# Setup work moved between the projections of a hybrid attention layer

## The chip, the cores and the metric

The kernel runs on one core of a Trainium2 chip. The metric is the time of one launch on the device in microseconds (us), as the median of several runs. A profile of one execution stands beside it.

Of the core's engines, TensorE (PE in the profile; PEld is its weight load) multiplies matrices and writes to PSUM, VectorE (DVE) and ScalarE (ACT) read PSUM and do the arithmetic between, GpSimd (POOL) takes part of the subtractions, and SyncE (SP) issues all transfers, in order, on one queue.

## The reference, cut to what matters

One layer of a streaming encoder on 2048 prompt tokens and 32 sample tokens of width 1024, in float32:

```python
z = rmsnorm(x, g_attn) @ w_in            # qa, ka, va (group A), qb, kb, vb (group B): 512 columns each
# A: differential attention, 4 heads, two maps of 64; bias from a T5 table, chunk-causal mask
lam = exp(sum(q1 * k1)) - exp(sum(q2 * k2)) + lam_init
oa = (softmax(s1 + bias) - lam * softmax(s2 + bias)) @ va
# B: band attention, 8 heads of 64; own chunk and 8 before; bias from a clipped table
ob = softmax(sb + band_bias) @ vb
h = x + concat(subnorm(oa), rmsnorm(ob)) @ w_out
h = h + square(relu(rmsnorm(h) @ w_up)) @ w_down
h = h + sigmoid(h @ w_ple_gate) * (p @ w_ple_proj)   # p: per-layer input, 256 wide
y = rmsnorm(h, g_final)
```

The keys and values are outputs too.

## The kernel before

Every float32 matmul is made of three with operands split in a high and a low part (`mm3`, lines 190 to 192): high by high, low by high and high by low. ScalarE or VectorE casts the high part, VectorE or GpSimd subtracts for the low one (`split`, L169, L171, L154, L164).

The tokens are cut into four blocks of 512 (the last has the 32 sample tokens too), in two halves. The normalised, transposed tokens of a block lie in two tiles, `aH` and `aL`. `prep` makes them, one token tile of 128 at a time: a load, a sum of squares, transposes (`rp`, `xp`), eight scalings (L345), a split.

`proj(half, grp, ..., vs, gs)` is a generator. It first makes the value columns in two pieces (`vs`: tiles `vps`, `vraw`, `vhl`), then for each of the four column groups (`gs`) the queries and the keys (`qps`, `qh`, `ql`, `kr`), and stores all of it to scratch in HBM (`vSa`, `vSb`, `qS`, `kS`). The key rows of the output are transposed back (`ktp`). The `qh` and `ql` tiles have two buffers each; the PSUM tiles of the projections, two as well.

The setup consists of three functions. `lam` works out lambda. `biases` multiplies one-hot tables (`oa`, `ob`) with the bias tables (`ta`, `tb`) into two rows (`pa`, `pb`), stores them (`ra`, `rb`) and spreads each row over 128 partitions by twelve copies from HBM to HBM (`dba`, `dbb`); attention loads its bias tiles from there. `prep_p` loads the per-layer input of each block (`pn`), transposes it on TensorE (`ppt`), splits it (`pph`, `ppl`, in the same buffers as `qh` and `ql`) and stores it to `pS`.

Then comes the first attention part: `attn_a` on the pairs of query tiles (0, 1), for each of the four heads, and again on (2, 3): two passes. Each step has score matmuls (`s`), a softmax on VectorE and ScalarE (`e`), transposes of the weights (`tpp`) and output matmuls (`o`). After it in the text come the group B projections of block 0, of block 1 with `prep` of block 2 woven in, the band attention `attn_b` (`sb`, `eb`, `tpb`, `ob`) on the first half, the projections of block 2 with `prep` of block 3, and so on; last the output projection, the MLP and the gate, which reads `pS`.

The order in which the engines meet all this isn't the order of the text. A scheduler with a timeline of its own sorts the instructions when the program is built: what stands earlier in the text has priority, and what stands later fills in where the earlier work waits by that timeline. So projections from further down run between the steps of attention. The order is fixed when the program runs; each engine takes its instructions strictly in that order. Pools with a fixed number of buffers set when a tile can be written again.

Of the kernel before, what the change touches and what calls it, by code (L numbers as in the profile page):

```python
# [41 lines left out]
HALVES = [(0, 1), (2, 3)]  # L42
# [40 lines left out]
def drain(gen):  # L83
    for _ in gen:
        pass
# [13 lines left out]
def weave(main, side, step, i=0, n=1):  # L99
    for _ in main:  # L100
        if i % step == 0:
            for _ in range(n):
                next(side, None)
        i += 1
    drain(side)
# [28 lines left out]
class Kern:  # L134
# [640 lines left out]
    def prep_p(self, sg, wk, ps):  # L775
        nc, a = self.nc, self.a
        for b in range(4):
            t0 = 512 * b
            n = BN[b]
            pn = wk.tile([P, 5, DPLE], F32, tag="pn", bufs=2, name="pn")  # L780
            self.dma(pn[:, :4], a["p_prompt"][0, 0, t0 : t0 + 512].rearrange("(i p) c -> p i c", p=P))
            if b == 3:
                self.dma(pn[:SS, 4], a["p_sample"][0, 0])
            for k in range(2):
                hi = sg.tile([P, BLK], F32R, tag="qh", bufs=2, name="pph")
                lo = sg.tile([P, BLK], F32R, tag="ql", bufs=2, name="ppl")
                pieces = [(0, 512)] + ([(512, SS)] if b == 3 else [])
                for c0, w in pieces:
                    tp = ps.tile([P, 512], F32, tag="tp", name="ppt")
                    for i in range(max(w // P, 1)):  # L790
                        m = min(w, P)
                        nc.tensor.transpose(
                            tp[:, P * i : P * i + m], pn[:m, c0 // P + i, P * k : P * k + P], self.ident[:m, :m]
                        )
                    nc.scalar.activation(hi[:, c0 : c0 + w], tp[:, :w], AF.Copy)
                    nc.vector.tensor_tensor(
                        lo[:, c0 : c0 + w], tp[:, :w], hi[:, c0 : c0 + w].bitcast(F32), op=ALU.subtract
                    )
                self.dma(self.pS[:, 0, k, t0 : t0 + n], hi[:, :n])
                self.dma(self.pS[:, 1, k, t0 : t0 + n], lo[:, :n])  # L800

    def raw_o(self, wk, k, t0, n):
        t = wk.tile([P, BLK], F32, tag="tmp", bufs=4, name="oraw")[:, :n]
        self.dma(t, self.oT[:, k, t0 : t0 + n])
        return t
# [290 lines left out]
    def run(self):  # L1096
        tc, nc, a = self.tc, self.nc, self.a
        with ExitStack() as top:

            def opened(stack, name, bufs, space=None, side="left"):  # L1100
                kw = {} if space is None else {"space": space}
                return stack.enter_context(
                    tc.tile_pool(name=name, bufs=bufs, side=side, reuse_waits="tile", **kw)
                )
# [5 lines left out]
            mm = opened(top, "mm", MM, PSUM)  # L1110
            tp = mm
            psx = ExitStack()
            ps_s = opened(psx, "pss", 5 - MM, PSUM, "right")
            ps_t = opened(psx, "pst", 2, PSUM, "right")
# [4 lines left out]
            sg = opened(s12, "sg", 2)  # L1119
            self.consts(cp)  # L1120
            with ExitStack() as x:
                pp = opened(x, "pp0", 3, side="right")
                acts = {b: self.actpair() for b in HALVES[0]}
# [1 line left out]
                    drain(self.prep(b, acts, pp, ps_s, "s"))  # L1125
            ppx = ExitStack()
            pp = opened(ppx, "pp", 1)
            drain(self.proj(HALVES[0], 0, acts, sg, mm, Rings((ps_t, "tp"))))
            with ExitStack() as x:
                wk = opened(x, "setup", 1, side="right")  # L1130
                self.lam(cp, wk)
                self.biases(wk, ps_t)
                self.prep_p(sg, wk, ps_t)
            self.small = True
            mark = tc.tile_snap_priority()
            with ExitStack() as x:
# [47 lines left out]
            wk = opened(sq_, "wk", 1)  # L1184
# [41 lines left out]
            wk = opened(top, "wk4", 1)  # L1226
# [79 lines left out]
```

## Time and profile before

| | us |
|---|---|
| median of three runs | 3257.93 |
| lowest, highest | 3256.70, 3264.15 |
| profiled execution | 3256.49 |
| its span | 3254.6 |

The profiled execution has its own time, 1.9 us above the span that the engines' rows cover. Times of rows are us from the span's start. A row of a window gives each engine's busy time and number of instructions, then TensorE's granted clock (1.00 is full speed), the mean busy share of the 16 DMA engines and GB/s. A row of a timeline gives start, duration, engine, line and operation; in brackets stands the idle time ahead of it and what ended it. `out<-in` are the program's tile names. Matmuls are pipelined: the distance between the starts of two neighbours is what one costs, and the duration is longer.

### The profile page before, as it was taken

Reading aid. Unit: us, or ns where it says so; the run is one execution under the profiler, and the core shown is the slowest. Engines: PE = TensorE matmul, PEld = TensorE weight load, DVE = VectorE, ACT = ScalarE, POOL = GpSimd, SP = SyncE. Lnnn points to the kernel's source line nnn. Section 1 sums busy time; section 2 is a strip of 40 time slices with the busy share of each in tenths; the row PEclk is TensorE's granted clock in tenths of the full one; section 3 lists DMA queues with packets and bytes.
Section 4 is the critical chain, followed back from the end, with each engine's and each line's share of the span. In section 5 each row is a group of like instructions: output and inputs, shape, how many; then the busy total and the mean of one; then the engine's idle time right before and its main releaser. Section 6 shows DMA issues by size and latency. Waiting matters only on the chain. (4 is left out here: it accounts for less than half of the span.)

```text
span 3254.6 us, 51557 instructions
## 1 busy us (share of the span) xinstructions
PE 3076.7 (95%) x17881; PEld 2692.7 (83%) x17881; DVE 1557.3 (48%) x3952; ACT 1693.7 (52%) x3717; POOL 1706.8 (52%) x2515
## 2 busy tenths in 40 slices
PE   6998999899999999999999999989899999999998
PEld 6877789789987887878788788868789999999988
DVE  5116786544465554676664565625442232223235
ACT  4226666776666765676665566544443222322245
POOL 5446766233245544565655455676854333433387
PEclk9999999999999999999999999999999999999999
DMA  7488786786788654554644544347531111111133
GB/s 232 165 259 246 226 244 206 213 259 202 215 239 229 187 146 118 152 156 138 199 122 135 137 123 136 121 143 233 150 113 46 46 46 46 46 46 46 47 94 103
DMA packets 519085, 489.02 MB, mean 150 GB/s; under 512 B 37885, under 2 KB 414017, under 8 KB 518825
## 3 DMA queue, kind: packets, MB, share of 16 engines
q1 hardware_dynamic: 518824, 485.73, 50.9%
q8 instruction: 142, 2.33, 0.3%
q14 instruction: 119, 0.97, 0.1%
HBM read 379.06 MB, written 110.49 MB: 150 GB/s over the span
## 5 line engine op out<-in xcount | busy, mean ns | idle before, releaser
L164 POOL TENSOR_TENSOR wl<-wr,wh 128x256 fp32r<-128x256 f32 x936 | 695.2, 774 | 489.4 <-ACT wh L169 453.1
L169 ACT ACTIVATE wh<-wr 128x1024 fp32r<-128x1024 f32 x338 | 357.2, 1057 | 598.5 <-PE dps L191 298.9
L971 DVE TENSOR_TENSOR h<-h,dps 128x512 f32<-128x512 f32 (+1 forms) x640 | 373.0, 585 | 575.0 <-PE dps L192 562.7
L154 POOL TENSOR_TENSOR wl<-wr,wh 128x256 fp32r<-128x256 f32 x416 | 301.8, 757 | 401.2 <-ACT wh L169 386.9
L190 PE MATMUL dps<-uh,wh 128*128 128x512 f32 (+1 forms) x1280 | 458.2, 358 | 7.1 <-DVE h L971 5.8
L190 PE MATMUL ups<-cH,wh 128*128 128x512 f32 (+1 forms) x1280 | 452.7, 354 | 5.7 <-ACT relu L936 4.5
L191 PE MATMUL ups<-cL,wh 128*128 128x512 f32 (+1 forms) x1280 | 451.5, 353 | 1.5 <-POOL cL L154 1.2
L192 PE MATMUL ups<-cH,wl 128*128 128x512 f32 (+1 forms) x1280 | 450.8, 352 | 0.0
L192 PE MATMUL dps<-uh,wl 128*128 128x512 f32 (+1 forms) x1280 | 450.1, 352 | 0.0
L191 PE MATMUL dps<-ul,wh 128*128 128x512 f32 (+1 forms) x1280 | 449.3, 351 | 0.0
L154 POOL TENSOR_TENSOR ul<-relu,uh 128x136 fp32r<-128x136 f32 (+1 forms) x320 | 198.9, 643 | 171.0 <-ACT uh L169 166.7
L190 PEld LDWEIGHTS dps<-uh,wh 128*128 128x128 f32 x1280 | 241.6, 189 | 39.7 <-DVE h L971 10.2
L190 PEld LDWEIGHTS ups<-cH,wh 128*128 128x128 f32 x1280 | 241.1, 188 | 38.6 <-ACT relu L936 4.7
L191 PEld LDWEIGHTS ups<-cL,wh 128*128 128x128 f32 x1280 | 241.6, 189 | 33.0 <-POOL cL L154 2.0
L192 PEld LDWEIGHTS dps<-uh,wl 128*128 128x128 f32 x1280 | 240.9, 188 | 33.6
L192 PEld LDWEIGHTS ups<-cH,wl 128*128 128x128 f32 x1280 | 241.3, 189 | 30.0
L191 PEld LDWEIGHTS dps<-ul,wh 128*128 128x128 f32 x1280 | 241.9, 189 | 26.5
L190 PE MATMUL qps<-aH,wh 128*128 128x512 f32 (+1 forms) x640 | 229.7, 359 | 11.0 <-ACT kr L432 3.4
L192 PE MATMUL qps<-aH,wl 128*128 128x512 f32 (+1 forms) x640 | 228.0, 356 | 0.0
L191 PE MATMUL qps<-aL,wh 128*128 128x512 f32 (+1 forms) x640 | 227.9, 356 | 0.0
L567 PE MATMUL s<-ka,q 128*128 128x256 f32 (+4 forms) x784 | 191.7, 346 | 30.8 <-DMA ka<-kS 10.1
L581 ACT ACTIVATE e<-s,nm 128x512 f32<-128x512 f32 (+3 forms) x256 | 154.9, 611 | 80.3 <-DVE nm L573 69.4
(218 smaller groups left out, 7075.0 us busy)
## 6 DMA issues: line engine op xcount, KB each, us to landing
wr<-w_up SPq DMA_DIRECT2D x96, 512.0 KB, 4.2
wr<-w_down SPq DMA_DIRECT2D x96, 512.0 KB, 3.8
wr<-w_in SPq DMA_DIRECT2D x74, 512.0 KB, 5.1
q<-qS SPq DMA_DIRECT2D x256, 128.0 KB, 4.3
v<-vSa SPq DMA_DIRECT2D x64, 512.0 KB, 3.9
ka<-kS SPq DMA_DIRECT2D x32, 512.0 KB, 7.7
wr<-w_out SPq DMA_DIRECT2D x32, 512.0 KB, 4.7
wr<-w_ple_gate SPq DMA_DIRECT2D x32, 512.0 KB, 4.4
```

The lines of the kernel that those rows point to most:

```text
L154: nc.gpsimd.tensor_tensor(out[:, sl], a[:, sl], b[:, sl], op=op)
L164: nc.gpsimd.tensor_tensor(out[:, sl], a[:, sl], b[:, sl], op=op)
L169: nc.scalar.activation(hi, raw, AF.Copy)
L190: nc.tensor.matmul(ps, lh, rh, start=start and i == 0, stop=False)
L191: nc.tensor.matmul(ps, lh, rl, start=False, stop=False)
L192: nc.tensor.matmul(ps, ll, rh, start=False, stop=stop and i == n - 1)
L567: nc.tensor.matmul(s, q[:, m, hl, P * qi : P * qi + nr], kt[:, m, k0 : k0 + n], start=hl == 0, stop=hl == 1)
L581: nc.scalar.activation(dst, src, AF.Exp, bias=nmx, accum_out=z[:nr, m, bi : bi + 1])
L971: nc.vector.tensor_tensor(hv, hv, ps, op=ALU.add)
```

## The change

`proj` of group A on the first half is cut in two: the value columns first, then `lam` and `biases`, then the query and key columns with `prep_p` woven in. For that `prep_p` becomes a generator that yields after each of its eight pieces, and `weave` advances it once for every second step of `proj`. Both calls of `proj` share one ring of PSUM tiles, and the pool `setup` is opened ahead of them.

```diff
                 self.dma(self.pS[:, 0, k, t0 : t0 + n], hi[:, :n])
                 self.dma(self.pS[:, 1, k, t0 : t0 + n], lo[:, :n])
+                yield
...
             pp = opened(ppx, "pp", 1)
-            drain(self.proj(HALVES[0], 0, acts, sg, mm, Rings((ps_t, "tp"))))
             with ExitStack() as x:
                 wk = opened(x, "setup", 1, side="right")
+                ring = Rings((ps_t, "tp"))
+                drain(self.proj(HALVES[0], 0, acts, sg, mm, ring, gs=()))
                 self.lam(cp, wk)
                 self.biases(wk, ps_t)
-                self.prep_p(sg, wk, ps_t)
+                weave(self.proj(HALVES[0], 0, acts, sg, mm, ring, vs=()), self.prep_p(sg, wk, ps_t), 2)
```

Nothing is added to or taken from the arithmetic or the transfers.

## The prediction

> **What bounds the kernel now.** I read the page first, then the table of windows of four microseconds around the place that is changed, then TensorE's and SyncE's rows in order of time there, and last the windows of the stages that follow.
>
> ```profile
> span 3254.6 us, 51557 instructions
> PE 3076.7 (95%) x17881; PEld 2692.7 (83%) x17881; DVE 1557.3 (48%) x3952; ACT 1693.7 (52%) x3717; POOL 1706.8 (52%) x2515
> ```
>
> TensorE is busy 95% of the span, and the change neither adds nor removes an instruction: on every engine the changed program holds the same instructions in another order. So time can only come from TensorE's idle stretches, from its clock, and from how well other work covers them. Around 208 us both are bad:
>
> ```profile
> core 0: us, PE busy (x) PEld busy (x) DVE busy (x) ACT busy (x) POOL busy (x), PEclk, DMA share, GB/s
> 192.00:200.00 8.00, 8.00 (x71) 8.00 (x70) 2.06 (x4) 3.86 (x6) 4.03 (x6) 1.00 0.63 213
> 208.00:212.00 4.00, 1.25 (x11) 1.05 (x9) 0.69 (x1) 1.19 (x2) 0.00 (x0) 1.00 1.06 392
> 212.00:216.00 4.00, 1.70 (x8) 1.32 (x8) 0.99 (x2) 0.00 (x0) 0.00 (x0) 0.73 1.09 362
> 216.00:220.00 4.00, 2.69 (x6) 2.15 (x7) 0.63 (x1) 2.04 (x4) 2.16 (x4) 0.50 1.11 344
> 220.00:224.00 4.00, 4.00 (x17) 3.25 (x16) 1.72 (x3) 1.81 (x3) 4.00 (x7) 0.92 0.98 361
> 248.00:252.00 4.00, 3.49 (x9) 2.80 (x10) 2.02 (x8) 3.26 (x8) 1.72 (x3) 0.58 1.07 249
> ```
>
> The transfers fill the DMA engines (share 1.06 to 1.11), TensorE starves, and then runs at half its clock. Its own rows show both:
>
> ```profile
> 208.85 0.28 PE L191 MATMUL vps<-wl,aH 128*128 128x256 f32 x1
> 208.97 0.27 PE L192 MATMUL vps<-wh,aL 128*128 128x256 f32 x1
> 213.58 1.70 PE L792 MATMUL ppt<-ident,pn 128*128 128x128 f32 x8 [4.33 <-DMA pn<-p_prompt]
> 217.31 0.80 PE L190 MATMUL qps<-aH,wh 128*128 128x512 f32 x1 [2.03 <-ACT vraw L383]
> 218.33 0.63 PE L192 MATMUL qps<-aH,wl 128*128 128x512 f32 x1
> 218.76 0.63 PE L190 MATMUL qps<-aH,wh 128*128 128x512 f32 x1
> 221.02 0.40 PE L190 MATMUL qps<-aH,wh 128*128 128x512 f32 x1
> 221.26 0.39 PE L191 MATMUL qps<-aL,wh 128*128 128x512 f32 x1
> ```
>
> Two waits, 4.33 us for the third load of the per-layer input and 2.03 us behind it; then two 512-wide matmuls stand 0.43 us apart, and from 221 us on 0.24 us. SyncE's rows say what filled the DMA engines:
>
> ```profile
> 58.66 0.45 SPq L145 DMA_DIRECT2D lv<-lambda_q  x1
> 65.19 0.35 SPq L145 DMA_DIRECT2D ob<-onehot_b  x1
> 68.97 0.56 SPq L145 DMA_DIRECT2D pn<-p_prompt  x1
> 195.36 5.41 SPq L145 DMA_DIRECT2D dbb<-rb  x8
> 205.97 1.75 SPq L145 DMA_DIRECT2D pn<-p_prompt  x2
> ```
>
> The loads of lambda, the one-hot tables and the first input tiles already go out at 58 to 71 us: the scheduler had hoisted them. What comes late is what hangs on matmuls of low priority: the eight copies that spread the band bias, and the input loads and stores behind them.
>
> **The change part by part.** In the program's order the first bias matmul moves from TensorE's position 902 to 361, inside the first value projections; the 34 transposes move from 945-1132 to 486-880, in bursts of four or five between query and key projections; and the first score matmul of the first attention part moves from position 1195 to 943, as nothing stands ahead of it any more. That last shift reaches on: the order differs up to position 11376 of 17878.
>
> *The stall at 209 us* goes: 4.33 + 2.03 = 6.4 us of waiting, and the lost clock, (1-0.73)·4 + (1-0.50)·4 + (1-0.92)·4 = 3.4 us. Together -9.8 us. Late next is the start of attention, which then meets lighter transfers.
>
> *The moved work itself* costs the same wherever it stands, as TensorE is the bound at both places:
>
> ```profile
> 183.97 0.80 PE L260 MATMUL pa<-oa,ta 32*4 32x384 f32 x2
> 186.91 1.88 PE L268 MATMUL pb<-ob,tb 128*8 128x512 f32 x4
> 192.48 0.60 PE L792 MATMUL ppt<-ident,pn 128*128 128x128 f32 x4
> 100.00:125.00 25.00, 25.00 (x114) 20.28 (x113) 3.09 (x5) 5.71 (x9) 10.40 (x15) 1.00 0.46 156
> ```
>
> At its new place TensorE is never idle, the DMA share is 0.46, and ScalarE and VectorE (5.71 and 3.09 of 25 us) have room for the evictions: 0.
>
> [...] The rows of 192 to 200 us hold 16 such transposes among dense matmuls, at a granted clock of 1.00. [...]
>
> *The new wait.* SyncE issues in order, and it waits for the bias rows and for the copies before it goes on (columns: total us, times, longest; for `pS`, KB and median us to landing):
>
> ```profile
> SPq L145 <- DMA dbb<-rb: 5.3, 8, 1.2
> SPq L145 <- DMA ra<-va_row: 2.4, 1, 2.4
> pS<-pph SPq DMA_DIRECT2D x6, 256.0 KB, 7.2
> 246.89 0.60 ACT L426 ACTIVATE qh<-qps 128x512 fp32r<-128x512 f32 x1 [2.30 <-DMA qS<-qh]
> 248.51 0.79 PE L190 MATMUL qps<-aH,wh 128*128 128x512 f32 x1 [2.57 <-ACT kr L432]
> ```
>
> In the changed order the first two query stores stand right behind the eight copies. The projections would begin near 89 us, the copies go out to about 100 us, and a store behind them landed after 7.2 us before: near 107 us. The third eviction needs that buffer (two of them, now shared with the input's halves) at 101 us, and TensorE, with two PSUM tiles, at 107 us. So it is borderline: from 0 up to what such a wait cost at 248 us, 2.57 us plus (1-0.58)·4 = 1.7 us of clock, 4.3 us. I take +1, near the lower end, by the 0.4 us that the working leaves it.
>
> *The stall at 248 us*, that same 4.3 us, arose with the DMA engines full. It may or may not come back where attention now starts: -4.3 to 0; half of it, -2.1. [...]
>
> *The first attention part* (score, transpose and output matmuls of `attn_a` on the first half, with projections between) runs in two passes over the heads. In the changed order the first pass has 655 positions instead of 600 and holds one token tile of `prep` instead of four; the second has 1145 instead of 1302 and eight instead of five.
>
> ```profile
> 241.50:358.00 116.50, 101.13 (x600) 88.72 (x599) 81.72 (x290) 75.38 (x230) 79.59 (x116) 0.93 0.85 244
> 358.00:577.00 219.00, 208.30 (x1352) 187.94 (x1351) 151.27 (x438) 147.44 (x402) 149.58 (x209) 0.98 0.77 222
> 300.00:325.00 25.00, 19.47 (x146) 17.94 (x145) 20.24 (x79) 17.91 (x62) 18.79 (x28) 0.96 0.77 230
> 425.00:450.00 25.00, 23.11 (x177) 21.92 (x176) 22.98 (x74) 19.37 (x60) 16.99 (x24) 1.00 0.82 234
> L345 DVE SCALAR_TENSOR_TENSOR a<-xp,g_attn_s,rb 128x128 f32<-128x128 f32 x32 | 8.9, 338 | 0.1
> ```
>
> Lost in the first pass: 15.4 us idle and 0.07·116.5 = 8.2 us of clock, 23.5 us on 93 us of work, a rate of 0.25. In the second: 10.7 + 4.4 = 15.1 us on 204 us, 0.074. The changed passes hold 93·655/600 = 102 and 204·1145/1302 = 179 us of work. With both at the low rate they lose 21 us instead of 38.6 (-18), with both at the high one 71 (+32). VectorE is why I stay between: eight scalings of 0.338 us make a token tile cost it about 3 us, so its share falls in the first pass (72 of some 118 us, 61%) and rises in the second (from 69% to about 161 of 200 us, 80%). The window at 425 us, in the second pass, has VectorE at 92% and loses only 1.9 of 25 us; that at 300 us, 81% and 5.5 us. I take rates of 0.16 and 0.12, 16 + 21.5 = 37.8 us: -1.
>
> *The band attention* comes after. Its first heads run with no projection between them for 222 TensorE instructions in the present order and for 334 in the changed one (position 2944 to 3278).
>
> ```profile
> 601.00:653.00 52.00, 38.71 (x229) 30.50 (x228) 37.83 (x163) 46.63 (x129) 2.33 (x16) 0.93 0.82 219
> 653.00:700.00 47.00, 42.11 (x325) 39.98 (x325) 23.95 (x87) 36.62 (x77) 23.23 (x40) 1.00 0.97 279
> ```
>
> The first row is that bare stretch: ScalarE is busy 46.63 of 52 us and sets the pace, TensorE idles 13.3 us and loses 3.6 us of clock, 16.9 us; counting each of its 229 instructions at the 0.12 us that stands between two 256-wide matmuls (208.85 to 208.97 us), 24.5 us. The second row, with projections between, loses 4.9 us on 325. So 112 more bare instructions cost 112/222 of 16.9 to 24.5 us, less 1.7 us that they lost anyway: 6.8 to 10.7 us. I take +9.
>
> **The sum:** -9.8 + 1 - 2.1 - 1 + 9 = -2.9 us. The profiled execution took 3256.5 us (its span 3254.6), the median of three runs is 1.4 us above it; so 3253.6 there, 3255 on the median. A difference under 0.3% (9.8 us) is what a measurement of this kernel cannot tell from no change. With no term at an extreme this case reaches from 3246 to 3266.
>
> **The rivals.**
>
> *The second pass chokes (slower).* Eight token tiles in 1145 positions push VectorE so far that the second pass loses at the first one's rate: 45.4 instead of 21.5 us, +23.9; with the band's bare stretch at its upper end (+1.7) the sum is +22.7: 3281 on the median. It turns the case to measurably slower from a loss of about 34 us in that pass. For it: the window at 300 us, where 81% of VectorE goes with 5.5 us of 25 lost. Against it: the one at 425 us.
>
> *Everything that starves is gone (faster).* Without the full DMA engines and with three tiles fewer in the first pass both passes lose at the low rate (-18), the stall at 248 us goes whole (-4.3), no new wait comes, the band costs +6.8: -9.8 - 18 - 4.3 + 6.8 = -25 us, 3233; with the first pass at 0.12 instead of 0.074, 3238. For it: the first pass lost most right behind the 209 us stall. Against it: its DMA share stays 0.77 at 300 us, where no setup is left.
>
> *Nothing moves that mattered.* The loads were hoisted already; if the copies only stall another stretch by as much, 3258. Against it: the share of 0.46 at the new place.
>
> [...]
>
> **How the numbers follow.** The forecast's own case 0.36, nothing moves 0.05, everything gone 0.28, the second pass chokes 0.29, the clock 0.02. The first two are within 0.3%: 0.41; faster 0.28; slower 0.31. Faster and slower cases hold more than half together, so the range takes in most of both, up to about the rivals' values: 3238 to 3279.
>
> **What would show it.** Right: no wait of TensorE for the input load after 200 us; the copies of the band bias issued before 102 us; clock 1.00 and TensorE full from 90 to 190 us; the first score matmul near 192 us; a bare band stretch of about 78 us with ScalarE near 90%. Wrong: a wait above 2 us at 100 to 110 us or a half-clock stretch before 190 us; a second pass that loses over 34 us or under 14; a bare stretch that loses no more than 17 us.

## The result, and the profile after

The changed kernel takes 3282.31 us (median of 6 runs, 3274.69 to 3289.89); the kernel before, measured beside it, 3259.45 us (6 runs, 3256.50 to 3264.15). The ratio is 1.0069, its 95% interval 1.0052 to 1.0086: slower by about 0.7%, or 23 us. The forecast was 3255 us with a range of 3238 to 3279, so it was wrong, in sign too. The profiled execution took 3278.81 us. Its page:

```profile
span 3276.7 us, 51585 instructions
PE 3093.2 (94%) x17881; PEld 2705.0 (83%) x17881; DVE 1547.0 (47%) x3952; ACT 1695.1 (52%) x3717; POOL 1703.6 (52%) x2515
```

TensorE is busy 16.5 us longer with the same 17881 instructions and idle 5.6 us longer: 22.1 us in all. So part of the loss is clock, part idle time, and neither total says where. I therefore give each kernel a loss by stage: for each pair of neighbouring matmuls the distance of their starts, less the usual distance for that shape and tile (the lower quartile in the kernel before), added up where positive. It holds idle time and lost clock together. Losses by stage, in us, read in the profiled execution of each kernel (the experiments' kernels are explained below):

| | to the first score matmul | first attention part | band attention | second attention part and what is left of the MLP to position 11380 | rest | sum | span |
|---|---|---|---|---|---|---|---|
| before | 39.0 | 58.0 | 88.1 | 74.0 | 75.8 | 334.9 | 3254.6 |
| before, again | 40.8 | 57.2 | 90.0 | 73.2 | 76.1 | 337.3 | 3256.8 |
| after | 33.5 | 51.4 | 110.7 | 88.3 | 72.9 | 356.8 | 3276.7 |
| after, again | 32.0 | 56.7 | 109.0 | 88.3 | 73.0 | 359.0 | 3278.9 |
| e1 own buffers | 26.0 | 64.0 | 97.6 | 92.9 | 71.7 | 352.2 | 3270.7 |
| e2 bias only | 32.0 | 67.5 | 94.2 | 84.3 | 71.2 | 349.2 | 3268.1 |
| e3 input only | 38.1 | 67.5 | 98.9 | 80.3 | 75.7 | 360.5 | 3280.0 |
| e4 hold | 31.2 | 66.6 | 98.1 | 75.4 | 75.9 | 347.2 | 3267.7 |
| e5 caches moved | 41.8 | 69.3 | 96.7 | 83.1 | 71.5 | 362.4 | 3281.3 |
| e12 cover, before | 40.7 | 55.8 | 86.1 | 75.6 | 72.9 | 331.1 | 3248.4 |
| e16 cover, change | 29.3 | 55.1 | 92.0 | 75.2 | 72.1 | 323.7 | 3241.8 |

The sums follow the spans: after against before +21.9 by stages, +22.1 by span. Two executions of one kernel differ by up to 7 us in a stage. By the table the change wins 5.5 us (8.8 in the second pair of executions) ahead of the first score matmul and 6.6 (0.5) in the first attention part, and loses 22.6 (19.0) in the band attention and 14.3 (15.1) behind it. The table ends the first attention part at its last transposes of the weights; the output matmuls behind them, which lose 5.3 us after (5.2 again) and 0.3 before, stand in the band's column. With them where they belong, the first attention part is -1.5 us (+4.5) and the band +17.3 (+14.1).

Now the places, in order of time. Some of SyncE's rows of the changed kernel:

```profile
93.56 0.29 SPq L145 DMA_DIRECT2D rb<-vb_row  x1
95.19 1.12 SPq L145 DMA_DIRECT2D dbb<-rb  x2
97.00 4.04 SPq L145 DMA_DIRECT2D dbb<-rb  x6
102.26 0.33 SPq L145 DMA_DIRECT2D qS<-qh  x1
111.03 0.73 SPq L145 DMA_DIRECT2D qS<-qh  x1
```

The band bias now goes out at 94 to 101 us, and the first query store stands behind it, at 102.26 us. What waits for that store, by the rows of ScalarE and VectorE, and then by TensorE's:

```profile
110.41 0.60 ACT L426 ACTIVATE qh<-qps 128x512 fp32r<-128x512 f32 x1 [13.43 <-DMA qS<-qh]
111.26 0.69 DVE L427 SCALAR_TENSOR_TENSOR ql<-qps,qh 128x512 fp32r<-128x512 f32 x1 [13.46 <-DMA qS<-ql]
```

```profile
107.26 0.60 PE L792 MATMUL ppt<-ident,pn 128*128 128x128 f32 x4
112.01 0.80 PE L190 MATMUL qps<-aH,wh 128*128 128x512 f32 x1 [4.15 <-DVE ql L427]
```

The eviction needs the `qh` buffer, which is free only when the store has landed, some 8 us after its issue; TensorE stands for 4.15 us, and the windows of the changed kernel show the clock behind it, then the two passes of the first attention part and the bare stretch of the band (same columns as in the prediction):

```profile
104.00:108.00 4.00, 3.86 (x19) 2.93 (x17) 0.00 (x0) 0.00 (x0) 0.00 (x0) 1.00 0.96 311
108.00:112.00 4.00, 0.00 (x0) 0.00 (x0) 0.74 (x2) 1.08 (x2) 0.00 (x0) 0.78 1.06 364
112.00:116.00 4.00, 3.99 (x9) 3.17 (x10) 0.29 (x1) 1.06 (x1) 2.73 (x4) 0.50 1.09 335
116.00:125.00 9.00, 9.00 (x40) 7.36 (x39) 1.22 (x2) 2.63 (x4) 5.36 (x9) 0.94 0.80 263
125.00:190.00 65.00, 65.00 (x303) 52.67 (x303) 10.93 (x19) 17.09 (x29) 22.24 (x32) 1.00 0.63 215
...
208.00:212.00 4.00, 4.00 (x36) 4.00 (x36) 1.79 (x9) 3.03 (x10) 3.50 (x5) 1.00 1.07 271
197.40:304.30 106.90, 102.42 (x657) 93.03 (x655) 70.81 (x255) 71.26 (x213) 75.47 (x111) 0.97 0.89 252
304.30:515.30 211.00, 189.34 (x1148) 166.03 (x1146) 158.34 (x465) 146.75 (x407) 145.81 (x202) 0.96 0.75 217
...
554.60:632.10 77.50, 58.18 (x336) 44.94 (x334) 51.01 (x220) 64.33 (x166) 2.63 (x18) 0.96 0.83 222
```

The stall at 208 us is gone. The first pass idles 4.5 us instead of some 15, the second 21.7 us instead of 10.7; by spacing the first loses 13.9 us (32.9 before), the second 42.7 (25.2 before). The same stretches of the kernel before, cut at its own first and last instructions:

```profile
242.60:359.20 116.60, 101.23 (x601) 88.81 (x600) 81.72 (x290) 75.77 (x231) 80.80 (x117) 0.93 0.85 245
359.20:570.40 211.20, 200.50 (x1293) 180.37 (x1292) 150.54 (x436) 145.10 (x397) 144.59 (x202) 0.98 0.77 223
603.40:655.90 52.50, 38.25 (x225) 30.01 (x223) 36.54 (x161) 44.69 (x125) 2.03 (x14) 0.93 0.83 225
```

The bare stretch holds 94 score matmuls instead of 64 and takes 77.5 us instead of 52.5: 0.82 us for each in both, with ScalarE busy 83% and 85%. Its loss grows from 26.4 to 38.9 us, 0.41 us for each score in both. Ahead of it, from the last weight transposes of the first attention part on, 12.5 us are lost, where it was 4.4. Of these, 5.3 us lie in the last output matmuls of the first attention part: TensorE waits for the low half of the weights, because VectorE, ahead of it, waits for GpSimd, and half-clock matmuls follow (0.21 us apart instead of 0.12):

```profile
511.49 0.93 DVE L667 SCALAR_TENSOR_TENSOR os<-os,g_sub_s,rsy 128x256 f32<-128x256 f32 x1 [3.10 <-POOL rsy L204]
```

```profile
513.07 0.58 PE L654 MATMUL o<-pL,v 128*128 128x256 f32 x1 [3.53 <-DVE pL L647]
```

The same wait is 3.5 us in the second execution; in the second pass of the kernel before the longest wait of this kind is 0.3 us.

Behind the band the second attention part (positions 6870 to 10839 after, 7226 to 11223 before) takes as long as before with 28 fewer instructions, and after it 541 instructions of the MLP are left to position 11380 where there were 157. The windows of the second part and of that rest in the changed kernel, and TensorE's waits in the rest (total us, times, longest):

```profile
1187.90:2010.40 822.50, 782.80 (x3970) 659.84 (x3969) 496.50 (x1116) 511.87 (x1186) 445.31 (x633) 0.98 0.51 141
2010.40:2140.40 130.00, 124.63 (x543) 100.28 (x542) 48.52 (x71) 50.85 (x75) 86.72 (x123) 0.99 0.41 130
```

```profile
PE dps L190 <- ACT relu L937: 2.9, 1, 2.9
PE dps L190 <- DVE h L972: 2.2, 3, 0.8
```

And the two windows in the kernel before:

```profile
1258.40:2081.80 823.40, 787.77 (x3998) 663.18 (x3997) 502.86 (x1120) 515.72 (x1191) 451.70 (x639) 0.99 0.51 142
2081.80:2115.40 33.60, 33.60 (x160) 27.54 (x159) 20.34 (x30) 17.44 (x31) 27.83 (x41) 1.00 0.52 161
```

The MLP that is left alone waits for its own evictions (5.4 us idle where there was none; a loss of 10.5 instead of 1.5 us), and the attention part loses 78.0 instead of 72.7 us.

### The profile page after: what moved, and what is told of

It reads as the page before. It is cut to its first block, busy times and chain, and to the rows that moved or that the text cites. A ratio compares the mean times of both kernels' runs of the same rounds, so it can differ in the third digit from the quotient of the medians.

```text
span 3276.7 us, 51585 instructions
## 1 busy us (share of the span) xinstructions
PE 3093.2 (94%) x17881; PEld 2705.0 (83%) x17881; DVE 1547.0 (47%) x3952; ACT 1695.1 (52%) x3717; POOL 1703.6 (52%) x2515
## 5 line engine op out<-in xcount | busy, mean ns | idle before, releaser
L191 PEld LDWEIGHTS ups<-cL,wh 128*128 128x128 f32 x1280 | 242.1, 189 | 32.4 <-POOL cL L154 1.3
L573 DVE TENSOR_REDUCE nm<-s 128x1 f32<-128x512 f32 (+3 forms) x256 | 147.3, 587 | 106.3 <-PE s L567 105.5
```

The costliest lines, as they stand in the source:

```text
L191: nc.tensor.matmul(ps, lh, rl, start=False, stop=False)
L573: nc.vector.tensor_reduce(nmx, s, axis=AX.X, op=ALU.max, negate=True)
```

## The experiments

Theory A: the change is slow because attention starts ahead of its work, so that projections have already run when the band's first heads and the end of the second attention part need something to stand between. (A' in two expectations is A, whatever set the order off.) Theory B: the setup at its new place does the harm, by the wait that it adds at 110 us. Theory C: any reshuffling of this tuned order costs about as much, whatever is moved. Differences are against the kernel before, measured beside each run.

**e1, own buffers.** The changed kernel with the halves of the per-layer input out of the shared buffers:

```diff
-                hi = sg.tile([P, BLK], F32R, tag="qh", bufs=2, name="pph")
-                lo = sg.tile([P, BLK], F32R, tag="ql", bufs=2, name="ppl")
+                hi = wk.tile([P, BLK], F32R, tag="pph", bufs=2, name="pph")
+                lo = wk.tile([P, BLK], F32R, tag="ppl", bufs=2, name="ppl")
```

> The changed kernel, but the halves of the per-layer input get tiles of their own instead of sharing the two buffers of the query and key halves. Theory A (most of the added time comes from the order of the work after the setup: second pass of the first attention part, bare band stretch, second attention part): only the wait at 107 us and its half-clock stretch go, 4.15 + 3.4 = 7.5 us; about 3275 us, still slower than before by 15 us. Theory B (the setup at its new place does the harm, by its copies and shared buffers, and the later differences follow from it): about 3260 us.

3272.19 us (3269.16 to 3279.94), ratio 1.0051 [1.0033, 1.0069]. Its windows at the place of the wait:

```profile
104.00:108.00 4.00, 4.00 (x21) 3.28 (x20) 0.00 (x0) 1.09 (x2) 0.00 (x0) 1.00 1.03 330
108.00:112.00 4.00, 4.00 (x19) 3.19 (x18) 1.03 (x2) 0.00 (x0) 1.24 (x2) 1.00 1.10 363
112.00:116.00 4.00, 4.00 (x21) 3.31 (x20) 0.00 (x0) 2.43 (x3) 2.20 (x4) 1.00 1.08 339
```

The wait and its half clock are gone, and the first stage loses 7.5 us less (6.0 less than in the changed kernel's second execution): that is the price of the new wait. But 14 us stay, near what was given for A, so theory B holds for 10 of the 23 us at most.

**e2 and e3, one part each.** e2 moves only lambda and the bias, e3 only the per-layer input:

```diff
 # e2
-                weave(self.proj(HALVES[0], 0, acts, sg, mm, ring, vs=()), self.prep_p(sg, wk, ps_t), 2)
+                drain(self.proj(HALVES[0], 0, acts, sg, mm, ring, vs=()))
+                drain(self.prep_p(sg, wk, ps_t))
 # e3
+                weave(self.proj(HALVES[0], 0, acts, sg, mm, ring, vs=()), self.prep_p(sg, wk, ps_t), 2)
                 self.lam(cp, wk)
                 self.biases(wk, ps_t)
-                weave(self.proj(HALVES[0], 0, acts, sg, mm, ring, vs=()), self.prep_p(sg, wk, ps_t), 2)
```

> Lambda and bias tables go behind the first value projections, the per-layer input stays behind all of the projections. Its program order has the first score matmul at position 1174 (before 1195, changed 943) and a bare band stretch of 253 instructions (222, 334). Theory A: it stays near before, 3255 to 3268 us, since attention starts as late. Theory B: the eight copies stand ahead of the first query stores as in the changed kernel, so 3270 us or more.

> The per-layer input is woven into the query and key projections, lambda and bias tables stay behind them. First score matmul at position 1104, bare band stretch 266. Theory A: between the two kernels, about 3262 to 3272 us. Theory B: without the copies ahead of the query stores no wait near 107 us, so no slower than before, 3250 to 3260 us.

e2: 3274.02 us, 1.0054 [1.0037, 1.0070]; e3: 3285.04 us, 1.0086 [1.0069, 1.0103]. Alone they cost some 16 and 27 us, where both together cost 23: the parts do not add up. e2's time is the one given for B, and e3's is above both that were given, so neither theory foresaw this pair. Both lose in the first attention part (67.5 us against 58.0) and in the band.

**e4 and e6, the later order held.** In the changed kernel the projections of group B on block 0 are put ahead of the first attention part, which gives the band its old length (bare stretch of 226 instructions, against 222) and the second part its old end (position 11223); e6 has e1's buffers too.

```diff
+            drain(self.proj((0,), 1, acts, sg, mm, tp, gs=range(4)))
             for js in JA0:
...
-            drain(self.proj((0,), 1, acts, sg, mm, tp))
+            drain(self.proj((0,), 1, acts, sg, mm, tp, vs=(), gs=()))
```

> The changed kernel, with all group B projections of block 0 written ahead of the first attention part in the text instead of behind it. The setup stands as in the changed kernel, but the order from the band attention on is nearly that of before: first band matmul at position 3251 in both, bare stretch 226 against 222, the end of the second attention part at 11223 in both, and the same instructions in the same order from position 7975 on. Theory A: the later terms go; the setup's own net of about -3 to -5 us is left, so 3250 to 3262 us. Theory B: the setup is unchanged, so 3275 us or more.

> The hold kernel with buffers of their own for the input's halves. Theory A': the wait near 107 us and its half clock go, as in the kernel with own buffers, 6 us off the hold kernel's 3270: about 3264 us. [...]

e4: 3270.30 us, 1.0050 [1.0032, 1.0068]; e6: 3275.76 us, 1.0043 [1.0028, 1.0058]. With the old end of the second part its loss is the old one: 75.4 us to position 11380, 1.5 of it in the MLP left over. That part of A holds. But the first attention part, now with other projections in it, loses 66.6 us, and the bare stretch 32.4, so e4 lies between the two times given. e6 missed its time (3264 us): the wait at 107 us went, and the first attention part lost 72.8 us instead.

**e5, another reshuffle.** In the kernel before, setup untouched, only `caches` (the stores of the key and value outputs) moves up in the text, ahead of the first band attention:

```diff
+            self.caches(sg, tp)
             acts[3] = self.actpair()
...
-            self.caches(sg, tp)
```

> The kernel before, setup untouched, with the small step that reads the caches written ahead of the first band attention in the text instead of behind it. The order is that of before up to about position 2050; then it reshuffles, with the first band matmul at 3137 (before 3251) and a bare stretch of 256 instructions (222). Theory A' (the order of the later stages carries the loss, whatever set it off): slower than before by 6 to 16 us, most of it in the second pass, the bare stretch and the second attention part. Theory B (the setup's place carries it): within 5 us of before.

3285.76 us, before 3262.20, 1.0074 [1.0057, 1.0090]: as much as the change under study, and more than the 6 to 16 us expected. TensorE's order is the same up to position 2050; the table has +11 us in the first attention part, +9 in the band, +9 behind it. Its last band instruction stands at position 7103 instead of 7226 and the second part ends at 11082 instead of 11223: it is shifted as the changed kernel is, only less.

**e7 and e8, the two kernels once more**, for the repeatability of the stages.

> The changed kernel once more, for a second trace. If its losses by stage belong to its order, the second pass (about 43 us lost), the bare stretch (39) and the second attention part (88) come out within 5 us each again; if they are a matter of where the half-clock windows fall, one of them moves by more than 8 us.

> The kernel before once more, for a second trace. If its losses belong to its order, first attention part 58, bare stretch 26 and second attention part 74 us come out within 5 us each again; otherwise as for the changed kernel.

3281.07 and 3258.55 us. Their stage rows stand in the table. In the changed kernel's second execution the second pass of the first attention part loses 48.3 us, a little more than 5 us off the first, and the bare stretch 35.2; in that of the kernel before they lose 24.4 and 27.8.

**e9, e10, e11, the stall taken away in the kernel before.** e9 gives the input loads four buffers, e10 gives the halves own buffers as well (e1's edit), e11 these alone.

```diff
-            pn = wk.tile([P, 5, DPLE], F32, tag="pn", bufs=2, name="pn")
+            pn = wk.tile([P, 5, DPLE], F32, tag="pn", bufs=4, name="pn")
```

> The kernel before, with four buffers instead of two for the loads of the per-layer input; nothing is moved in the text. All four loads then stand at 69 to 80 us in SyncE's order, and the later order stays close to that of before (first score matmul 1200 against 1195, first band matmul 3251, bare stretch 226 against 222, the same from position 7975 on). If the stall at 209 us is what there was to win, and the order what there was to lose: the 4.33 us wait and its half clock go, 6 to 10 us, less up to 3 us for two loads of 512 KB more in the full stretch at 70 to 80 us: about 3252 us against 3259. If any new order loses 10 to 20 us: 3262 us or more.

> The same with buffers of their own for the input's halves; the order is that of before from position 3814 on, and 0.986 of the positions between 3251 and 11376 hold the same instruction. The waits on the shared buffers at 215 and 248 us (2.03, 2.57 us) can go too: 3248 to 3254 us. If the first attention part's order alone decides, it may lose up to 10 us there instead: 3260 us.

> The kernel before with the input's halves in buffers of their own, two input loads at a time as before. Order as before from position 3814 on. The wait for the input load at 209 us stays; the waits on shared buffers go: 3255 to 3261 us. With the order of the first attention part against it, up to 3268 us.

3269.20 us (1.0034 [1.0021, 1.0047]), 3268.21 (1.0030 [1.0018, 1.0041]) and 3279.54 (1.0064 [1.0049, 1.0078]). None gains; e9 falls under the second of its two cases, e10 and e11 lie above every time given. TensorE's waits from 205 to 225 us, e9 and then e10:

```profile
PE ppt L792 <- DVE ppl L796: 3.4, 2, 2.9
```

```profile
PE ppt L792 <- DVE ppl L796: 5.2, 2, 4.4
```

The wait for the load has become a wait for the split of the half before it: the stall formed again one step on. The first stage loses 40.4, 41.3 and 38.4 us, as before (39.0), and the new order behind it costs 10 to 22 us.

**e12 and e13, cover for the band's first heads.** If theory A is right, projections must be left when the band starts. The text's order is changed so that the projections of blocks 2 and 3 and the caches stand ahead of the first band attention; e12 does it in the kernel before, e13 in the changed kernel with e1's buffers.

```diff
-            for js in JB[: len(JB) // 2]:
-                self.attn_b(js, bp, ps_s, ps_t, ps_o)
...
+            for js in JB[: len(JB) // 2]:
+                self.attn_b(js, bp, ps_s, ps_t, ps_o)
```

> The kernel before with the projections of blocks 2 and 3 and the caches written ahead of the first band attention instead of between its two halves, so that the scheduler has projections to put between the band's first heads; TensorE's order is the same up to position 3251, and no run of 40 band instructions without a projection is left there (a run of 101 is left at position 5197). If missing cover is the cause of the bare stretch's loss: that loss falls from 26 us to 8 us or less, and the time to 3240 to 3255 us. If the order as such decides (every other order tried was slower, this one moves 8,000 positions): 3265 us or more, with the loss at another place. If ScalarE's pace in attention decides whatever stands between: 26 us are lost there still, the time within 5 us of before.

> The changed kernel with own buffers for the input's halves (as e1_own) and the same swap as e12_cover: no bare run of 40 or more at the band's first heads. If missing cover is the cause: against e1_own's 3272 us the bare stretch gives back 25 to 30 us and the last multilayer-perceptron work some 8 us, less what the longer covered stretch loses: 3240 to 3255 us. If the order as such decides: 3262 to 3285 us.

e12: 3254.40 us (10 runs), before 3262.76 (25 runs), 0.9975 [0.9963, 0.9988]. e13: 3245.78 us (6 runs), 0.9943 [0.9924, 0.9961]. Theory C's times (3262 and more) did not come. e13 against e1: the band's loss goes from 97.6 to 86.5 us, that behind it from 92.9 to 70.4. In e12 the time is in the range given, but not by the way given: the old bare stretch is covered, a bare run of 101 instructions further down loses 16.5 us, and the band as a whole only 2 us less. So the swap by itself is worth little in the kernel before, and much in the changed one: there it takes away the excess.

**e16 and e18, the change alone with cover, and e13 once more.** e16 is the changed kernel with the same swap and nothing else.

> The changed kernel with the projections of blocks 2 and 3 and the caches ahead of the first band attention, and the input's halves in the shared buffers as in the change (e13_cover_own without its own buffers). Against e12_cover (3254.4 us) it is the change alone, with cover in both. If missing cover is what made the change slow: the stall at 209 us (10 us) is won and the wait at 110 us (7.5 us) paid, so 3248 to 3257 us, some 7 us above e13_cover_own. If the change is slow of itself: 3270 us or more.

> e13_cover_own once more, for its interval: if its 0.9943 was no chance, 0.992 to 0.997 again, and some 7 us below e16_cover_change in the same call.

e16: 3243.70 us (6 runs, 3238.10 to 3256.79), before 3261.93 (17 runs), 0.9950 [0.9934, 0.9966]; e18: 3247.29 us, 0.9952 [0.9940, 0.9964]. Both beat the kernel before by some 0.5%, and e16 lies 39 us below the changed kernel. e16 is better than any time given for it, and e18 lies above it, not 7 us below. Windows of e16 at the new wait, at the band's first heads, and from the band's end:

```profile
104.00:108.00 4.00, 1.25 (x8) 0.83 (x6) 0.49 (x1) 1.09 (x2) 0.00 (x0) 1.00 1.04 369
108.00:112.00 4.00, 3.75 (x11) 2.99 (x12) 0.53 (x2) 1.06 (x1) 2.20 (x4) 0.66 1.12 334
...
590.00:650.00 60.00, 56.38 (x433) 54.74 (x431) 24.24 (x95) 38.86 (x98) 25.13 (x47) 0.97 0.80 237
...
1280.70:2100.20 819.50, 784.50 (x3975) 660.88 (x3976) 509.85 (x1126) 517.14 (x1193) 452.13 (x638) 0.98 0.52 143
2050.00:2107.60 57.60, 57.04 (x300) 47.97 (x299) 37.77 (x87) 39.44 (x89) 37.24 (x51) 1.00 0.39 123
```

The wait at 106 us is still there. At the band's first heads TensorE is busy 56.38 of 60 us, where it was 58.18 of 77.5. The second part ends at position 11346 of 11380, and what is left from there to 11380 loses 1.2 us. The change with cover on both sides, e16 against e12, is worth 8 us by the ratios (0.9950 and 0.9975 of 3262, whose intervals just touch) and 10.7 by the medians; by the table it wins 11.4 us ahead of the first score matmul and loses 5.9 in the band, with the rest within 1 us. The own buffers brought nothing here: e13 and e18 lose less in the first stage (25.7 and 25.6 us) and more in the first attention part (61.7 and 68.3).

**e14, e15 and e17, more TensorE work in the bare stretch.** e14 does the score matmuls of the first four token tiles of the band twice, e15 their transposes twice, e17 the same transposes in the changed kernel.

```diff
 # e14
-                for hl in range(2):
+                for hl in range(4 if t is not None and t < 4 else 2):
 # e15, e17
-                for x, (i, kn) in enumerate(ch):
+                for x, (i, kn) in enumerate(ch * (2 if t is not None and t < 4 else 1)):
+                    x %= len(ch)
```

(In e14 the operand index and the start and stop flags are taken modulo 2.)

> The kernel before with every score matmul of the first four token tiles of the band attention done twice (128 more, each into a tile that is then written again; the output is unchanged). At some 0.12 us each they cost 15 us where TensorE is the bound, and nothing in a stretch that ScalarE paces. If the half clock of the bare stretch comes from too few matmuls, the granted clock there rises from 0.93 towards 1.00 and the time changes by -3 to +5 us; if each costs its time: +15 us, 3273 us; if the order decides, more.

> The kernel before with the transposes of the probabilities of the first four token tiles of the band attention done twice (the output is unchanged; a bare stretch of about 250 instructions stays). [...]

> The changed kernel with the transposes of the probabilities of the first four token tiles of the band attention done twice (bare stretch of 345 instructions instead of 334). If a stretch short of TensorE work falls to half clock and more transposes lift it, as e15_transposes_twice's bare stretch ran at clock 1.00: the loss there falls by 8 us or more from 38.9 us, the time to 3265 to 3275 us. If that was chance: 3282 us or some 5 us more.

e14: 3269.42 us, 1.0023 [1.0011, 1.0035], between the times given. The kernel holds 64 more matmuls, not the 128 of the expectation; at 0.12 us each that is 7.7 us, and 6.7 were measured: they cost their time, because the scheduler then puts projections in and the bare stretch is gone (the band loses 83.8 us, 4 less than before). e15: 3258.45 us, 0.9988 [0.9978, 0.9999]; e17: 3257.92 us, 0.9991 [0.9982, 1.0000]. With 80 instructions more, the changed kernel is 24 us faster, better than either time given. The bare stretches of e15 and then e17, of e4, and of the second executions of the kernel before and of the changed kernel, a line for each:

```profile
606.50:651.10 44.60, 37.41 (x253) 30.99 (x252) 33.09 (x145) 39.18 (x114) 1.75 (x12) 1.00 0.91 239
```

```profile
558.20:623.20 65.00, 53.92 (x347) 44.45 (x345) 45.34 (x200) 55.90 (x148) 2.32 (x16) 0.97 0.85 223
```

```profile
604.60:663.70 59.10, 45.49 (x230) 37.46 (x228) 36.16 (x163) 46.98 (x127) 2.03 (x14) 0.77 0.70 197
```

```profile
604.30:658.20 53.90, 41.61 (x226) 33.01 (x224) 35.41 (x160) 44.40 (x124) 2.04 (x14) 0.87 0.81 218
```

```profile
558.00:631.70 73.70, 57.55 (x336) 44.67 (x334) 51.08 (x220) 64.27 (x166) 2.61 (x18) 0.95 0.88 236
```

Counted in the traces, e15's stretch holds 54 scores in 44.6 us, e17's 82 in 65.0: 0.83 and 0.79 us for each, the old pace. (e15's clock is 1.00 where the kernel before had 0.93, and its stretch is 7.9 us shorter than the 52.5 us there.) The added transposes are free there, where ScalarE is the busiest engine (88% and 86%); the stretch is shorter because the scheduler leaves fewer scores bare (64 to 54, 94 to 82). Behind the band e17 loses 74.6 us, as the kernel before, where the changed kernel loses 88.3. Theory A does not explain that: the second part ends at position 10958 instead of 10839, but 80 of these 119 positions are the added transposes. Counted in the traces, 3006 matmuls of the output projection and the MLP stand ahead of e17's last weight transposes, 2967 in the changed kernel and 3351 in the kernel before. So e17 has nearly as little left to cover attention with, and does not pay for it; why is open.

## Why the prediction was wrong

*The stall at 209 us* went, as forecast, and nothing waits there (the row 208:212).

*The moved work* is free: the clock is 1.00 from 125 to 190 us, with 26 of the 34 transposes woven in there. So the clock did not fall at them, the case given 0.02.

*The new wait* came at the forecast place and by the forecast chain, but above the forecast's upper end: 6.8 us by spacing (6.3 in the second execution) instead of +1, with a bound of 4.3. The wait of 4.15 us and the half clock of 112 to 117 us make this up; the clock that was lost while TensorE waited costs nothing more. The prediction's sums of waits and lost clock count that part twice: the stall at 209 us was 9.1 us by spacing in the execution that it read, not 9.8. What was mis-sized is the landing: 7.2 us after issue was the median of the stores to `pS` before; here the two buffers were free only at 110.4 us, 8.2 us after the issue and behind eight copies. A wait "borderline by 0.4 us" was sized by the margin, when the row for such a wait at 248 us already showed what it costs once it comes. Ahead of the first score matmul the sum was -8.8 us; measured, -5.5 and, in the second pair of executions, -8.8.

*The first attention part*: forecast -1 and, for the stall at 248 us, -2.1; with its last output matmuls, -1.5 was measured, and +4.5 in the second pair. The net is near by luck, for its parts aren't: the first pass won 19 us, and the second, which was to lose 21.5 us, lost 42.7, some 17.5 more than before. By its size that is the rival that chokes (45.4 us). The rival's reason is not shown: VectorE is busy 158.34 of the pass's 211 us, 75% and not 80%, and was at 71% before; and behind the longest wait, the one that ends at 513 us, VectorE was itself waiting for GpSimd. The rival's time, 3281 us, is nearly the measured one, but it had that pass alone in it: with the first pass's gain the two cancel, and the time came from elsewhere.

*The bare stretch*: forecast +9, bound 10.7; measured +12.5, and +7.4 in the second pair. The length was 77.5 us against 78 forecast. ScalarE was at 83%, not near 90%.

*The step that failed* is what the sum left out. The prediction says that the order differs up to position 11376, and prices that shift only at the bare stretch; everything else behind the first attention part stood at nothing, without a row for it. Measured: +2.8 us between the first attention part and the bare stretch, +2 in the rest of the band, +14.3 in the second attention part and the MLP left over, -3 in the rest: some +16 us, and +19 in the second pair. The terms that the sum did hold make up the other 8 us of the error (6 in the second pair). e16 shows the other side: with cover at the band's start the change is worth 8 to 11 us, near the forecast's own -9.8 for the stall, though partly by chance (-11.4 us ahead of the first score matmul, +5.9 in the band). So the forecast had the change's own place about right, and the order behind it wrong.

Of the theories, B is worth some 7 us where it is seen, and nothing in the end where cover is there. That the order behind the change carries the verdict is shown by e16, e18 and e13: with the same setup and another order behind it the change gains, and in e16 the band's column loses 19 us less than in the changed kernel and the stage behind it 13 less. That missing cover is the reason, theory A, fits these and e4 (old end, old loss of the second part), but not e17, which has nearly as little cover behind the band and loses no more than the kernel before. So A is supported and not shown. C is not needed for the verdict and is refuted as a rule, since e12, e13 and e16 are reshuffles that gain; but e5, e9, e10 and e11 show that an order shifted by no setup at all, or by one buffer, costs 10 to 24 us as well.

What stays open: why the first attention part loses 62 to 73 us in several orders (e1 to e6, e10, e11, e13 and e18 among them, e6 with 72.8 and e11 with 72.1) and 51 to 59 in others with nearly the same instructions; and what took the loss behind the band away in e17.

## What to carry to other kernels

Where a scheduler fills the waits of one stage with the work of another, that work is a stock: what starts a consumer earlier or frees a stall spends the stock earlier, and the bill can come at a stage that then stands bare, here some 400 us after the change with 94 scores bare instead of 64; for the loss 1,900 us after it this reading is not shown. So follow a shift to the last position that it reaches and count at each stage what is left to cover it (0.37 to 0.43 us for each bare score in the four executions of the two kernels), before the stall's gain is booked. And where the forecast leaves a shifted stage at nothing, widen the range: orders alone were worth 3244 to 3286 us here. And a removed stall is only removed when its next waiter is free (in e9 and e10 it formed again one step on, with waits of 3.4 and 5.2 us): look at the store that must land before the next buffer can be written, and take the price of such a wait whole where the margin is within its spread.

## What the runs showed of the hardware

In the bare stretches, where ScalarE was the busiest engine (79% to 87% of the stretch), the pace changed little with TensorE's clock: 0.82 us a score at a granted clock of 0.93 (before) and 0.96 (after), 0.84 and 0.78 in their second executions at 0.87 and 0.95; at 0.77 (e4, 59.1 us for 68 scores) it is 0.87 us.

Doubled transposes did not lower the clock in such a stretch: in e15 it was 1.00 where the kernel before had 0.93 and 0.87, and in e17 0.97 where the changed kernel had 0.96 and 0.95. The transposes' part of those two stretches, e15 and then e17 (TensorE's busy time and instructions of the tile `tpb`, clock, DMA share, GB/s):

```profile
606.50:651.10 44.60, 15.73 (x122) 1.00 0.91 239
```

```profile
558.20:623.20 65.00, 22.06 (x159) 0.97 0.85 223
```

They are 122 of 253 and 159 of 347 instructions there. Without doubling the granted clock was 0.77 to 0.96 in these stretches; what sets it there isn't settled by these runs.
